# Activation split in eight steps behind evacuations, token-half pairs, an early pool for the first block product, and reordered phase-change loads

## The chip, the cores and the metric

The kernel runs on one core of a Trainium2 chip. The metric is device time in microseconds (us), the median of several executions. The profile is of one further execution, taken by the hardware profiler.

## What is computed

One layer on 1024 tokens of width 1024: an FFN, a mixer (stick-breaking attention beside RWKV-7), a second FFN, each between two RMS norms and added to the residual stream. The change touches the two FFNs alone (inner width 2816):

```python
def swiglu(x, w_gate, w_up, w_down):
    return (jax.nn.silu(x @ w_gate) * (x @ w_up)) @ w_down
# x = x + 0.5 * rmsnorm(swiglu(rmsnorm(x, pre_g), w_gate, w_up, w_down), post_g)
```

## The kernel before

Every fp32 product is three matmuls (`mm3`, L118 to L121): an operand is split into a rounded part "hi" and a remainder "lo" (fp32r), and hi x hi, hi x lo, lo x hi are added up in PSUM. Making hi is a cast on ACT (or POOL), making lo a subtraction on DVE (or POOL).

*Up-projection (`Ffn.up`).* The 2816 inner channels are 22 blocks of 128. Blocks 0 and 1 are done plainly (`plain_mm`, `plain_evac`), and their activations are stored, split, to DRAM (`hf`). Blocks 2 to 21 use a 2 x 2 Strassen scheme (Winograd's form) over halves of the depth, halves of the tokens and the gate and up weights: seven products n = 1..7 of 12 matmuls each instead of eight. `combine` makes the seven activation operands once, from the normed input (sums of 128x2048 on DVE: R, H, L). `prep(f)` makes a block's seven weight operands, hi and lo, on DVE (sums S), ACT and POOL (wh, wl); it is called one block ahead. `load(f)` brings the raw gate and up weights (r0, r1). `product(f)` runs the seven on PE in the order X n1, Z n2, DY n5, X n6, DW n4, X n7, DY n3. Three of them go to bank X one on top of the other: ACT must copy p out of it between n1 and n6, u between n6 and n7, and v after n7. Sums and the gated products on DVE then make the block's activations in both token halves.

*The split.* These activations are split again, for the down-projection, and stored. For blocks 2 to 17 two neighbouring blocks make one Strassen operand set of seven (`split_pair`, to `hs`); blocks 18 to 21 are split plainly (`split_plain`, to `hl`). Both are generators: `split_step()` runs one piece, at seven places in `product(f)`. A pair is queued after its odd block, so its steps run in the even block that follows. Whether an instruction keeps the place in which it is written is a scheduler's decision: it orders every engine's program ahead of time.

*Down-projection (`ffn_down`).* First the two plain blocks (`df`, 96 matmuls from `hf`, weights W split by POOL), then four groups of four blocks by Strassen (`prep(c)` makes the weights from four tiles B, with sums T, on POOL and ACT; PE runs `dX`, `dY`, `dZ`), then blocks 18 to 21 plainly. SP issues nearly all DMAs, in order: one that waits holds up all behind it.

Pools: `fu` holds the raw weights of even blocks, S, and the activations; `WP` those of odd blocks and most wh/wl pairs; `st` is one ring of six 128x512 tiles for hi, lo and one sum.

Of the kernel before, what the change touches and what calls it, by code (L numbers as in the profile page):

```python
# [30 lines left out]
def layer_kernel(ctx: ExitStack, tc: tile.TileContext, a: dict, out: bass.AP, dbg=None):  # L31
# [183 lines left out]
    class Ffn:  # L215
# [138 lines left out]
        def split(self, src, hi, lo, dst, eng=None):  # L354
            nc.scalar.copy(hi, src)
            nc.vector.tensor_tensor(lo, src, hi, op=ALU.subtract)
            for x, t in enumerate((hi, lo)):
                (eng or nc.sync).dma_start(dst(x).rearrange("i p t -> p i t"),
                                  t.bitcast(F32).rearrange("p (i t) -> p i t", t=P))

        def st(self, name, dt=F32R):
# [1222 lines left out]
```

## Time and profile before

| what | value |
|---|---|
| median of 3 runs | 2334.72 us (2334.41 to 2335.84) |
| the profiled execution | 2340.09 us, its span 2338.3 us |
| TensorE (PE) busy in the span | 2140.4 us, 92% |
| products of FFN1 on PE | 103.22 to 531.34 us |
| products of FFN2 on PE | 1664.94 to 2093.01 us |
| Strassen part of the down-projection begins | 570.01 us and 2133.24 us |

An engine's idle stretch counts only where PE waits for it. A timeline row gives the start, the length, engine, line, operation, output and input tiles with shapes, and in brackets the idle time before it and what ended that. Tile names lose their block numbers in the profile: f1u is u of any block of FFN1.

### The profile page before, as it was taken

How to read it: one execution, taken by the hardware profiler on the slowest of the kernel's cores; microseconds unless marked ns; L12 is line 12 of the kernel's file. 1: busy time of each engine (PE TensorE's matmuls, PEld its weight loads, DVE VectorE, ACT ScalarE, POOL GpSimd, SP SyncE). 2: the span in 40 equal slices, each digit the busy share in tenths (PEclk: the TensorE clock that was granted, in tenths of full speed). 3: DMA queues.
4: the chain of work that ended last, by engine and by line, in shares of the span. 5: the costliest groups of instructions: out<-in, count | busy, mean ns of one | idle time of the engine just before them, and what ended most of it. 6: DMA issues, size and time to landing. Idle time of an engine off the chain costs nothing. (4 is left out here: it accounts for less than half of the span.)

```text
span 2338.3 us, 30308 instructions
## 1 busy us (share of the span) xinstructions
PE 2140.4 (92%) x10976; PEld 1756.4 (75%) x10976; DVE 1296.4 (55%) x1900; ACT 823.3 (35%) x1429; POOL 1058.0 (45%) x899
## 2 busy tenths in 40 slices
PE   7689999997999999999999999898699999989998
PEld 5567777786888777677888887777577777767886
DVE  5765654641555655735526768556656546532555
ACT  4323333323112544324136657335233233332202
POOL 2266555557562354344311111221565555556742
PEclk8899999998999999999989889999899999999999
DMA  4244454448766353353665562442344545547765
GB/s 123 66 126 123 131 149 117 136 139 274 238 204 203 99 162 117 109 167 112 211 147 162 155 197 88 153 136 90 90 122 135 144 117 146 147 143 243 248 212 171
DMA packets 415476, 353.83 MB, mean 151 GB/s; under 512 B 35168, under 2 KB 337248, under 8 KB 415328
## 3 DMA queue, kind: packets, MB, share of 16 engines
q1 hardware_dynamic: 402512, 345.35, 49.5%
q10 hardware_dynamic: 12816, 6.56, 1.1%
q8 instruction: 87, 1.43, 0.3%
q14 instruction: 61, 0.50, 0.1%
HBM read 224.96 MB, written 126.88 MB: 150 GB/s over the span
## 5 line engine op out<-in xcount | busy, mean ns | idle before, releaser
L314 POOL TENSOR_TENSOR f1wl<-f1r,f1wh 128x512 fp32r<-128x512 f32 x100 | 138.9, 1400 | 101.4 <-ACT f1wh L311 98.1
L314 POOL TENSOR_TENSOR f2wl<-f2r,f2wh 128x512 fp32r<-128x512 f32 x100 | 138.7, 1398 | 94.1 <-ACT f2wh L311 90.9
L107 POOL TENSOR_SCALAR wh<-wr 128x1024 fp32r<-128x1024 f32 x55 | 64.9, 1180 | 243.9 <-PE wod L121 57.2
L108 POOL TENSOR_TENSOR wl<-wr,wh 128x1024 fp32r<-128x1024 f32 x55 | 136.9, 2491 | 21.2 <-PE f1dY L121 18.0
L512 DVE TENSOR_TENSOR f2acc<-f2dX,f2acc 128x512 f32<-128x512 f32 x64 | 44.3, 692 | 81.0 <-PE f2dX L121 81.0
L512 DVE TENSOR_TENSOR f1acc<-f1dX,f1acc 128x512 f32<-128x512 f32 x64 | 44.3, 691 | 79.4 <-PE f1dX L121 78.7
L313 POOL TENSOR_SCALAR f2wh<-f2r 128x512 fp32r<-128x512 f32 x60 | 46.2, 777 | 88.1 <-PE f2X L120 35.4
L313 POOL TENSOR_SCALAR f1wh<-f1r 128x512 fp32r<-128x512 f32 x60 | 46.1, 774 | 87.1 <-PE f1X L120 36.0
L458 DVE TENSOR_TENSOR f2y<-f2X,f2y 128x512 f32<-128x512 f32 x20 | 13.8, 691 | 115.9 <-ACT f2v L457 115.9
L458 DVE TENSOR_TENSOR f1y<-f1X,f1y 128x512 f32<-128x512 f32 x20 | 13.8, 691 | 115.8 <-ACT f1v L457 115.8
L1408 POOL TENSOR_SCALAR a_0B<-a_512B 128x1 f32<-128x1 f32 x32 | 14.1, 440 | 138.3 <-DVE a_512B L1409 110.3
L119 PE MATMUL pj<-x1X4h,wh 128*128 128x512 f32 x176 | 76.6, 435 | 0.0
L119 PE MATMUL pj<-x1X2h,wh 128*128 128x512 f32 x176 | 72.6, 412 | 0.6 <-DVE qkl L1119 0.5
L121 PE MATMUL pj<-x1X4h,wl 128*128 128x512 f32 x176 | 72.2, 410 | 0.0
L120 PE MATMUL pj<-x1X4l,wh 128*128 128x512 f32 x176 | 70.7, 402 | 0.0
L121 PE MATMUL pj<-x1X2h,wl 128*128 128x512 f32 x176 | 69.5, 395 | 0.0
L120 PE MATMUL pj<-x1X2l,wh 128*128 128x512 f32 x176 | 69.1, 393 | 0.0
L119 PE MATMUL f1X<-X_1h,f1wh 128*128 128x512 f32 x80 | 37.3, 466 | 25.4 <-ACT f1u L451 25.4
L119 PE MATMUL f2X<-x2X4h,f2wh 128*128 128x512 f32 x80 | 36.9, 461 | 23.4 <-ACT f2u L451 23.4
L314 POOL TENSOR_TENSOR f1wl<-f1S,f1wh 128x512 fp32r<-128x512 f32 x40 | 56.4, 1417 | 4.0 <-ACT f1wh L311 2.4
L314 POOL TENSOR_TENSOR f2wl<-f2S,f2wh 128x512 fp32r<-128x512 f32 x40 | 55.9, 1404 | 4.0 <-ACT f2wh L311 2.4
L540 POOL TENSOR_TENSOR f2dwl<-f2B,f2dwh 128x1024 fp32r<-128x1024 f32 x20 | 47.5, 2401 | 18.4 <-ACT f2dwh L539 18.4
(1472 smaller groups left out, 7247.2 us busy)
## 6 DMA issues: line engine op xcount, KB each, us to landing
f1ho<-f1hs_d SPq DMA_DIRECT2D x112, 256.0 KB, 4.0
f2ho<-f2hs_d SPq DMA_DIRECT2D x112, 256.0 KB, 3.3
f1hs_d<-f1sh SPq DMA_DIRECT2D x56, 256.0 KB, 2.8
f1hs_d<-f1sl SPq DMA_DIRECT2D x56, 256.0 KB, 2.5
f2hs_d<-f2sh SPq DMA_DIRECT2D x56, 256.0 KB, 2.8
f2hs_d<-f2sl SPq DMA_DIRECT2D x56, 256.0 KB, 2.5
wr<-in_w_in_dram SPq DMA_DIRECT2D x27, 512.0 KB, 3.9
f1r<-in_ffn_w_gate_dram SPq DMA_DIRECT2D x20, 512.0 KB, 4.4
```

Of the source, the lines that this page charges most:

```text
L107: nc.gpsimd.tensor_scalar(wh, raw, 1.0, 0.0, op0=ALU.mult, op1=ALU.add)
L108: nc.gpsimd.tensor_tensor(wl, raw, wh, op=ALU.subtract)
L119: nc.tensor.matmul(ps, lhsT=lh, rhs=rh, start=first, stop=False, **kw)
L120: nc.tensor.matmul(ps, lhsT=lh, rhs=rl, start=False, stop=False, **kw)
L121: nc.tensor.matmul(ps, lhsT=ll, rhs=rh, start=False, stop=last, **kw)
L313: nc.gpsimd.tensor_scalar(wh, src[n], 1.0, 0.0, op0=ALU.mult, op1=ALU.add)
L314: nc.gpsimd.tensor_tensor(wl, src[n], wh, op=ALU.subtract)
L458: nc.vector.tensor_tensor(y5, x, y5, op=ALU.add)
L512: nc.vector.tensor_tensor(quarter(tt, n), ps, quarter(tt, n), op=ALU.add)
L540: nc.gpsimd.tensor_tensor(wl, src[n], wh, op=ALU.subtract)
L1408: nc.gpsimd.tensor_scalar(B[:, w:w + 1], iv, 1.0, 0.0, op0=ALU.mult, op1=ALU.add)
```

## The change

- `split_pair` becomes a list of seven casts with the subtractions and sums one step behind, eight steps in all; its instructions and those of `split_plain` are kept in program order. `product` calls `split_step` at five places, each behind an evacuation.
- The ring `st` becomes three: `sh` (3), `sl` (2), `s1` (1); a block's activations are two 128x512 tiles (the former v and y) instead of one of 128x1024.
- A pair joins token tile i with i + 4 (halves) instead of 2i with 2i + 1, in the stores and in the down-projection.
- Raw weights of even blocks and S move to a pool `fr` that is open before the plain blocks; `load(2)` is issued on ACT's queue, and `prep(2)` is called before the last plain evacuations.
- In `ffn_down`, W, B's first tiles and all of hf are asked for at the top; hf gets a place of its own; eight hl stores move from ACT's queue to SP's. Five of the thirteen t4 tiles come from a pool that is opened later.

```diff
-            pool, tag = (WP, "wr") if f % 2 else (self.fu, "raw")
+            pool, tag = (WP, "wr") if f % 2 else (self.fr, "raw")
...
-                nc.sync.dma_start(t, w[:, :, c])
+                (nc.scalar if f == 2 else nc.sync).dma_start(t, w[:, :, c])
...
+        def hi(self, nm, n, src):
+            t = self.fu.tile("sh", f"{self.nm}h{nm}{n}", [P, HT], F32R)
+            tc.keep_in_program_order(nc.scalar.copy(t, src))
+            return t
+
+        def tt(self, dst, a_, b_, op):
+            tc.keep_in_program_order(nc.vector.tensor_tensor(dst, a_, b_, op=op))
...
+            steps = ((1, A11, (S, A21, A22, ALU.add)), (2, A12, (A21, A11, A21, ALU.subtract)),
+                     (4, A22, (A11, S, A11, ALU.subtract)), (5, S, (A12, A12, A11, ALU.subtract)),
+                     (7, A21, None), (6, A11, None), (3, A12, None))
+            held = None
+            for n, src, nxt in steps:
+                hi = self.hi(f, n, src)
+                if held is not None:
+                    lo(*held)
+                held = n, src, hi
+                if nxt is not None:
+                    self.tt(*nxt)
+                yield
+            lo(*held)
...
             self.mm(f, 1, "X")
+            self.mm(f, 2, "Z")
+            self.evac1(f)
             self.split_step()
-            self.mm(f, 2, "Z")
-            self.split_step()
-            self.evac1(f)
             y = self.mm(f, 5, "DY")
...
+            self.fr = Pool(self.nm + "r", dict(raw=2, S=1))
+            self.load(2)
             comb = self.combine()
...
             self.plain_mm(1, 1)
             next(comb)
+            self.prep(2)
             self.plain_evac(0, 1)
             self.plain_evac(1, 1)
             next(comb, None)
-            self.fu = Pool(self.nm + "u", dict(raw=2, S=1, wh=1, wl=1, tp=6, hv=2, st=6))
-            self.load(2)
+            self.fu = Pool(self.nm + "u", dict(wh=1, wl=1, tp=3, hv=6, sh=3, sl=2, s1=1))
             self.load(3)
-            self.prep(2)
...
+        W = [weight(F.wd[:, 0:2, n * 512:(n + 1) * 512], 2, 512, False) for n in range(2)]
         acc = [pl.t4(f"{nm}acc{tt}") for tt in range(NT)]
         rp = Pool(nm + "rp", dict(wh=6, wl=6, rw=5, T=2), "right")
+        B0 = blocks(0)
+        hp = Pool(nm + "hp", {}, "right")
+        hf = hp.const(f"{nm}hf", [P, NT, 2, 2, P], F32R)
+        for tt in range(NT):
+            nc.sync.dma_start(hf[:, tt].bitcast(F32), F.hf[tt])
...
-            a_, b_ = 2 * i, 2 * i + 1
+            a_, b_ = i, i + 4
```

ACT in block 14 (even) of FFN1 before, from the copy of p to that of u (f1sh are the split's casts, f1wh weight casts, f1hv activations):

```order
L434 COPY f1p14_2623<-f1X14_2586 128x512
L384 CAST f1sh79_2620<-f1hv13_2554 128x512
L384 CAST f1sh81_2646<-f1hv13_2554 128x512
L311 CAST f1wh_47_2569<-f1S15_2557 128x512
L436 ACTIVATE f1p14_2623<-f1p14_2623 128x512
L384 CAST f1sh83_2667<-f1s177_2601 128x512
L384 CAST f1sh85_2687<-f1hv12_2414 128x512
L447 COPY f1y14_2640<-f1DY14_2627 128x512
L384 CAST f1sh87_2709<-f1hv12_2414 128x512
L384 CAST f1sh89_2727<-f1hv13_2554 128x512
L311 CAST f1wh_48_2575<-f1r1_15_2446 128x512
L451 COPY f1u14_2661<-f1X14_2586 128x512
```

The same stretch of ACT in the change, where f1h121 is the cast of operand 1 of the pair that begins with block 12:

```order
L419 COPY f1p14_2603<-f1X14_2577 128x512
L312 CAST f1wh_47_2560<-f1S15_2548 128x512
L421 ACTIVATE f1p14_2603<-f1p14_2603 128x512
L368 CAST f1h121_2608<-f1v12_2364 128x512
L431 COPY f1y14_2624<-f1DY14_2611 128x512
L368 CAST f1h122_2626<-f1v13_2528 128x512
L312 CAST f1wh_48_2566<-f1r1_15_2426 128x512
L435 COPY f1u14_2645<-f1X14_2577 128x512
```

Of six split casts two are left between the two copies; the others went behind u or into the odd block.

DVE at the end of `combine` before (f1L4 and X1_1l are its last remainders, f1e the plain activations, f1S2 the first sum of block 2's weights):

```order
L266 TENSOR_TENSOR f1R2_580<-f1R3_581,f1R2_580 128x2048
L251 TENSOR_TENSOR f1L4_577<-f1R1_579,f1H4_576 128x2048
L356 TENSOR_TENSOR f1e0_1_647<-f1e0_1_647 128x512
L350 TENSOR_TENSOR f1e1_1_654<-f1pZ1_1_616,f1e1_1_654 128x512
L251 TENSOR_TENSOR X1_1l_129<-f1R2_580,X1_1h_128 128x2048
L356 TENSOR_TENSOR f1e1_1_654<-f1e1_1_654 128x512
L302 TENSOR_TENSOR f1S2_675<-f1r1_2_669 128x512
L303 TENSOR_TENSOR f1S2_675<-f1S2_675,f1r0_2_667 128x512
```

The same stretch of DVE in the change:

```order
L267 TENSOR_TENSOR f1R2_587<-f1R3_588,f1R2_587 128x2048
L252 TENSOR_TENSOR f1L4_584<-f1R1_586,f1H4_583 128x2048
L304 TENSOR_TENSOR f1S2_654<-f1S2_654,f1r0_2_505 128x512
L305 TENSOR_TENSOR f1r1_2_507<-f1r0_2_505,f1r1_2_507 128x512
L309 TENSOR_TENSOR f1r0_2_505<-f1r0_2_505,f1S2_654 128x512
L351 TENSOR_TENSOR f1e0_1_681<-f1pZ0_1_534,f1e0_1_681 128x512
L351 TENSOR_TENSOR f1e1_1_688<-f1pZ1_1_623,f1e1_1_688 128x512
L252 TENSOR_TENSOR X1_1l_129<-f1R2_587,X1_1h_128 128x2048
L357 TENSOR_TENSOR f1e0_1_681<-f1e0_1_681 128x512
L357 TENSOR_TENSOR f1e1_1_688<-f1e1_1_688 128x512
```

Block 2's sums (its first, f1S2 from r1_2, stands six rows above these) now come ahead of the last remainder and of the plain activations of the second token half.

SP at the change of phase of FFN1 before (wr are plain down weights, f1B the Strassen ones, f1hf the plain activations; the hl stores of blocks 20 and 21 are on ACT's queue):

```order
L104 DMA wr5_3810<-in_ffn1_w_down_dram 128x2x512
L104 DMA wr6_5199<-in_ffn1_w_down_dram 128x2x512
L104 DMA wr7_5211<-in_ffn1_w_down_dram 128x2x512
L526 DMA f1B000_3818<-in_ffn1_w_down_dram 128x2x512
L526 DMA f1B001_3820<-in_ffn1_w_down_dram 128x2x512
L526 DMA f1B011_3822<-in_ffn1_w_down_dram 128x2x512
L526 DMA f1B010_3824<-in_ffn1_w_down_dram 128x2x512
L526 DMA f1B100_4018<-in_ffn1_w_down_dram 128x2x512
L555 DMA f1hf0_3858<-f1hf_d_120 128x512
```

SP at the same place in the change:

```order
L105 DMA wr6_5183<-in_ffn1_w_down_dram 128x2x512
L105 DMA wr7_5195<-in_ffn1_w_down_dram 128x2x512
L362 DMA f1hl_d_122<-f1h200_3672 128x4x128
L362 DMA f1hl_d_122<-f1v20_3622 128x4x128
L362 DMA f1hl_d_122<-f1h201_3692 128x4x128
L362 DMA f1hl_d_122<-f1y20_3573 128x4x128
L501 DMA f1hf_3807<-f1hf_d_120 128x512 x8
L520 DMA f1B00_3800<-in_ffn1_w_down_dram 128x2x512
L362 DMA f1hl_d_122<-f1h210_3756 128x4x128
L362 DMA f1hl_d_122<-f1v21_3736 128x4x128
L362 DMA f1hl_d_122<-f1h211_3761 128x4x128
L362 DMA f1hl_d_122<-f1y21_3687 128x4x128
L520 DMA f1B01_3801<-in_ffn1_w_down_dram 128x2x512
```

hf moved ahead of B, and the four hl stores of block 21 stand between B's first tile and its other three.

## Rows read from the trace of the kernel before

**Rows 1.** the page's busy time, share of the span and instructions of each engine

```profile
PE 2140.4 (92%) x10976; PEld 1756.4 (75%) x10976; DVE 1296.4 (55%) x1900; ACT 823.3 (35%) x1429; POOL 1058.0 (45%) x899
```

**Rows 2.** PE's waits from 103 to 535 us: us in total, times, longest

```profile
PE f1X L119 <- ACT f1u L451: 25.4, 10, 3.0
```

**Rows 3.** PE's waits from 1660 to 2100 us

```profile
PE f2X L119 <- ACT f2u L451: 23.4, 9, 3.2
```

**Rows 4.** stretch: us, busy PE, PEld, DVE, ACT, POOL; clock, DMA share, GB/s

```profile
103.30:531.40 428.10, 400.11 (x1680) 325.29 (x1680) 243.14 (x293) 134.11 (x240) 259.75 (x222) 0.96 0.46 128
...
293.10:296.50 3.40, 3.33 (x9) 2.67 (x10) 2.46 (x3) 0.02 (x1) 1.31 (x1) 0.56 0.79 217
```

**Rows 5.** PE's timeline around one wait: start, us, what it is

```profile
287.46 0.39 PE L119 MATMUL f1DW<-f1H,f1wh 128*128 128x512 f32 x1
...
289.95 0.39 PE L121 MATMUL f1DW<-f1H,f1wl 128*128 128x512 f32 x1
293.17 0.79 PE L119 MATMUL f1X<-X_1h,f1wh 128*128 128x512 f32 x1 [2.83 <-ACT f1u L451]
293.76 0.63 PE L120 MATMUL f1X<-X_1l,f1wh 128*128 128x512 f32 x1
```

**Rows 6.** ACT's timeline in an odd block (one row), then an even one

```profile
268.62 0.59 ACT L451 COPY f1u<-f1X 128x512 f32<-128x512 f32 x1 [0.76 <-PE f1X L121]
...
287.57 0.64 ACT L436 ACTIVATE f1p<-f1p 128x512 f32<-128x512 f32 x1 [4.68 <-DVE f1p L435]
...
291.50 0.62 ACT L384 CAST f1sh<-f1hv 128x512 fp32r<-128x512 f32 x1 [1.26 <-DVE f1sl L389]
...
292.54 0.58 ACT L451 COPY f1u<-f1X 128x512 f32<-128x512 f32 x1
```

**Rows 7.** timelines of DVE (two rows) and POOL in that even block

```profile
285.16 1.77 DVE L404 TENSOR_TENSOR f1hv<-f1s,f1hv 128x512 f32<-128x512 f32 x1
286.86 0.68 DVE L435 TENSOR_TENSOR f1p<-f1Z,f1p 128x512 f32<-128x512 f32 x1
...
276.61 0.63 POOL L313 TENSOR_SCALAR f1wh<-f1S 128x512 fp32r<-128x512 f32 x1 [1.73 <-PE f1DY L120]
277.32 1.29 POOL L314 TENSOR_TENSOR f1wl<-f1S,f1wh 128x512 fp32r<-128x512 f32 x1
...
284.65 1.73 POOL L314 TENSOR_TENSOR f1wl<-f1S,f1wh 128x512 fp32r<-128x512 f32 x1
```

**Rows 8.** timelines where products start: PE, DVE, POOL; last PE in FFN2

```profile
103.22 0.79 PE L119 MATMUL f1X<-X_0h,f1wh 128*128 128x512 f32 x1 [16.98 <-POOL f1wh L313]
...
93.63 2.28 DVE L251 TENSOR_TENSOR X_1l<-f1R,X_1h 128x2048 fp32r<-128x2048 f32 x1
...
100.34 1.26 POOL L314 TENSOR_TENSOR f1wl<-f1r,f1wh 128x512 fp32r<-128x512 f32 x1 [74.71 <-ACT f1wh L311]
...
1664.94 0.80 PE L119 MATMUL f2X<-x2X2h,f2wh 128*128 128x512 f32 x1 [17.20 <-POOL f2wh L313]
```

**Rows 9.** the page's DMA issues: KB each, median us to landing

```profile
f1hs_d<-f1sh SPq DMA_DIRECT2D x56, 256.0 KB, 2.8
...
f1r<-in_ffn_w_gate_dram SPq DMA_DIRECT2D x20, 512.0 KB, 4.4
```

**Rows 10.** timelines where down-projections start: PE (four rows), POOL, ACT

```profile
543.16 0.76 PE L119 MATMUL f1df<-wh,f1hf 128*128 128x512 f32 x1 [11.82 <-DMA f1hf<-f1hf_d]
...
570.01 0.39 PE L119 MATMUL f1dX<-f1dwh,f1ho 128*128 128x512 f32 x1
...
2104.67 0.77 PE L119 MATMUL f2df<-wh,f2hf 128*128 128x512 f32 x1 [11.66 <-DMA f2hf<-f2hf_d]
...
2133.24 0.39 PE L119 MATMUL f2dX<-f2dwh,f2ho 128*128 128x512 f32 x1
...
537.78 2.34 POOL L529 TENSOR_TENSOR f1T<-f1B,f1B 128x1024 f32<-128x1024 f32 x1
...
551.91 1.04 ACT L539 CAST f1dwh<-f1B 128x1024 fp32r<-128x1024 f32 x1 [5.95 <-POOL f1B L536]
```

More of the change, by code (lines that the diff above doesn't have):

```diff
@@ L43, in __init__ @@
             self.bufs = bufs
+            self.more = None
         def close(self):
@@ L54, in t4 @@
         def t4(self, name, shape=None, dt=F32, tag="t4"):
-            return self.tile(tag, name, shape or [P, 1024], dt)
+            return (self.more or self).tile(tag, name, shape or [P, 1024], dt)
         def t2(self, name, shape=None, dt=F32, tag="t2"):
@@ L351, in plain_evac, with split, put @@
             self.split(hv, s.bitcast(F32R), hv.bitcast(F32R), lambda x: self.hf[4 * h:4 * h + 4, :, x, f, :])
-        def split(self, src, hi, lo, dst, eng=None):
+        def split(self, src, hi, lo, dst):
             nc.scalar.copy(hi, src)
             nc.vector.tensor_tensor(lo, src, hi, op=ALU.subtract)
-            for x, t in enumerate((hi, lo)):
-                (eng or nc.sync).dma_start(dst(x).rearrange("i p t -> p i t"),
+            self.put(dst, hi, lo)
+        def put(self, dst, *parts):
+            for x, t in enumerate(parts):
+                nc.sync.dma_start(dst(x).rearrange("i p t -> p i t"),
@@ L500, in up, with blocks @@
             self.fu.close()
+            self.fr.close()
     def ffn_down(pl, F, gb, post, half=None, nextx=None):
         nm = F.nm
+        def blocks(c):
+            f0 = FS + 4 * c
+            return [v2(rp.tile("rw", f"{nm}B{c}{x}", [P, 1024])) for x in range(4)]
+        v2 = lambda t: t.rearrange("p (k e) -> p k e", k=2)
+        W = [weight(F.wd[:, 0:2, n * 512:(n + 1) * 512], 2, 512, False) for n in range(2)]
         acc = [pl.t4(f"{nm}acc{tt}") for tt in range(NT)]
         rp = Pool(nm + "rp", dict(wh=6, wl=6, rw=5, T=2), "right")
+        B0 = blocks(0)
[3 more added lines that the diff above has]
+            nc.sync.dma_start(hf[:, tt].bitcast(F32), F.hf[tt])
         quarter = lambda tt, n: acc[tt][:, n * 512:(n + 1) * 512]
-        v2 = lambda t: t.rearrange("p (k e) -> p k e", k=2)
         nslot = [0]
@@ L518, in slot, with prep @@
             return [v2(pool.tile(t, f"{nm}d{t}{i}", [P, 1024], F32R)) for t in ("wh", "wl")]
-        def prep(c):
+        def prep(c, tiles):
             f0 = FS + 4 * c
-            first = slot()
             B = {}
-            for kh, e in ((0, 0), (0, 1), (1, 1), (1, 0)):
-                B[kh, e] = v2(rp.tile("rw", f"{nm}B{c}{kh}{e}", [P, 1024]))
+            for t, (kh, e) in zip(tiles, ((0, 0), (0, 1), (1, 1), (1, 0))):
+                B[kh, e] = t
                 nc.sync.dma_start(B[kh, e], F.wd[:, f0 + kh:f0 + kh + 4:2, e * 512:(e + 1) * 512])
@@ L548, in hload @@
             return ho
-        W = [weight(F.wd[:, 0:2, n * 512:(n + 1) * 512], 2, 512, False) for n in range(2)]
-        prep(0)
+        prep(0, B0)
         for tt in range(NT):
-            h2 = pl.tile("ho", f"{nm}hf{tt}", [P, 2, 2, P], F32R)
-            nc.sync.dma_start(h2.bitcast(F32), F.hf[tt])
+            h2 = hf[:, tt]
             for n in range(2):
@@ L627, in ffn_down @@
         EX[0] = None
+        pl.more.close()
         ex.close()
```

84 lines of the change are left out of this document (23 added, 61 removed).

## The prediction

> **What bounds the kernel now.** I first read the page's table of engines: TensorE (PE) is busy for 92% of the span, DVE 55%, POOL 45%, ACT 35% [rows 1]. So the time is PE's, and two things can shorten it: fewer matmuls (the change leaves their number alone) or fewer gaps between them. The second view is PE's waits in the two up-projections: on the ACT copy that makes u, FFN1 waits 10 times for 25.4 us [rows 2], FFN2 9 times for 23.4 us [rows 3]. The third is busy time by stretch: from 103.30 to 531.40 PE has 1680 matmuls in 428.1 us [rows 4].
>
> The floor: from 287.46 to 289.95 [rows 5] eleven distances of matmuls make 2.49 us, 0.2266 each. A block has 7 products of 12 matmuls, 84 x 0.2266 = 19.03 us; 20 blocks are 380.7 us. So the stretch is 47.4 us over its floor, 4.7 us for each of the ten even blocks. [Rows 5] show one of them: 2.83 us of waiting, then matmuls of 0.63 us instead of 0.39; the granted clock from 293.1 to 296.5 is 0.56 [rows 4], close to the lower of its two levels (1.2 and 2.4 GHz). A wait thus costs itself and nearly 2 us of slow matmuls.
>
> Why u is late: [rows 6] are ACT in that even block. X n6 ends where n4 begins, at 287.46; n4 takes 2.72 us, and then PE wants the bank again, but the copy of u only runs at 292.54. Before it stand silu (287.57, waiting for DVE's p), four casts of the split, y's copy and a weight cast; one cast at 291.50 waits for a DVE subtraction. DVE did split work first and came to p at 286.86, one step of it stretched to 1.77 us [rows 7]. In the odd block, where no split is queued, the copy stands at 268.62, in time.
>
> **The change, part by part.**
>
> *1. The split in eight steps, tied behind evacuations.* A pair of blocks still has 7 casts, 7 subtractions, 4 sums, and no matmul more or less. Between the copies of p and u, ACT had ten instructions in an even block, six of them split casts; now it has six with two. DVE makes p before it touches the split. Silu, cast, y's copy, cast and weight cast at 0.52 us (291.50 to 292.54 is two) put u 1.0 to 1.6 us ahead of PE's need, and no cast there waits for a subtraction of its own step. Five steps fall in the even block, three in the odd. So the ten waits go, with their slow matmuls. Bounds of what is left in an FFN: 0, or 1.5 us in each of 20 blocks, 30 us (the nearest row is the stretched DVE operation, 1.77 - 0.68 = 1.1 us, once or a little more per block). I take 3 us, near the low end, because the slack covers one such stretch.
>
> *The doubt in it: DVE beside POOL.* In [rows 7] POOL's subtraction takes 1.29 us, and 1.73 where DVE works too. A pair of blocks asks DVE for 23 operations with both inputs in SBUF (8 for the weights, 11 for the split, 4 products): 23 x 0.68 = 15.6 us. It asks POOL for 14 subtractions and 8 casts: 14 x 1.29 + 8 x 0.63 = 23.1 us. Sum 38.7 us, against PE's 38.07. In the old order the even block alone asks for 17 x 0.68 + 11.55 = 23.1 us against 19.03, which is why DVE came late there. Were the two engines wholly exclusive, a pair would take 0.7 us more than PE's floor. POOL's operation from 284.65 ends at 286.38, and DVE's from 285.16 ends 0.55 us after it. The Trainium skill ("SBUF — State Buffer", section "Who interferes with whom") says that two such operations exclude each other for a whole instruction; by that rule, the trace agrees at this place, and rival (b) below would hold.
>
> *2. Block 2 prepared early.* Today POOL's first subtraction for it stands at 100.34 and PE's first product at 103.22 after 16.98 us of waiting [rows 8]. The change issues its two loads on ACT's queue, among the last scalings of the input at about 67 us; with 4.4 us to land [rows 9] they are there at 72. POOL is idle, so what n1, n2, n5 and n4 need is ready before the plain blocks end at 103.22 - 16.98 = 86.24, and PE goes on at once. The price: four DVE operations of 0.6 us, all before the last sum, which ended at 95.91 [rows 8] and now ends near 99; only n7 reads it, now the last product of the block. X n6 waits for p's copy, behind two casts on ACT: 97.9 instead of 97.1, 0.9 us. Block 3's loads still stand behind hf's stores: last store near 100.5, landing 2.8 us and load 4.4 us [rows 9], cast and subtraction 0.63 + 1.29 [rows 7], so 109.6 where PE comes at 106.1: 3.5 us, and slow matmuls after it 1.6 us, by [rows 5]. Sum 6 us, of the old 17. Bounds 3 (loads land at once) and 11 (four DVE sums stretched by 1.1 us each). FFN1's products then end at 86.24 + 380.7 + 6 + 3 = 475.9 instead of 543.16 - 11.82 = 531.34 [rows 10]: 55.4 us. FFN2's plain part ends at 1664.94 - 17.20 = 1647.74 [rows 8]; 1647.74 + 389.7 = 2037.4 instead of 2104.67 - 11.66 = 2093.01: 55.6 us.
>
> *3. The start of the down-projection.* Now PE waits 11.82 us for hf, has 96 plain matmuls (floor 21.75 us) and comes to the Strassen part at 570.01, 38.7 us after the products; in FFN2 40.2 us [rows 10]. The change loads hf into a place of its own when n4 of the last block is over, 8 us before the end, so the hf wait goes. But only B's first tile is issued before the last hl stores; the other three stand behind them, and these wait for the block's evacuation, 6 us after the end: B lands 10.5 us after it. POOL's first T stood 6.4 us after the end, at 537.78, and each step takes 2.34 us: T moves 4 us later, and ACT's cast at 551.91 (20.6 us after the end), which waits for the fourth difference, to 24.6. PE's eleventh plain group needs an ACT copy behind that cast: 26.4, and its last five groups take 5 x 6 x 0.2266 = 6.8: 33.2 us after the end. Gain 5.5 and 7.0 us. Bounds: 0 (POOL's chain is late by all that PE gains) and 11.8 (the hf wait goes, nothing takes its place); the value lies between them, where the chain of rows puts it.
>
> Eight hl stores move from ACT's queue to SP's; the four of the last block are costed here by what stands behind them in SP's order. The Trainium skill ("DMA: Bandwidth & Descriptors", section "Issuing engines are not separate DMA queues") has it that the choice of engine saves only issue time; by that, the move is free and this gain is nearer 11.8 than 5.5 us. No row of before shows the stores on SP; I keep the order's answer.
>
> *4. The rest.* Token-half pairs change where stores go, not how many there are. Buffers shrink: 3 for hi and 2 for lo, where six were shared. Two lo buffers turn in two steps, 7.6 us in an even block; a store lands in 2.8 us [rows 9], so I cost it at nothing. The mixer, the Strassen part and the tail keep their instructions.
>
> **Sum.** 55.4 + 55.6 + 5.5 + 7.0 = 123.5 us. The profiled execution took 2340.09 us (its span is 2338.3), so 2216.6; the median, 2334.72, is 5.4 us less: 2211 us.
>
> **Rivals.**
> - *(a) The wait only moves.* A cast held up by DVE or POOL keeps u late once a pair. 19 waits at 4.4 us (the stretch's 47.4 us less the 3 assumed, over ten) are 84 us, less the 6 taken: 2289; with half of them, 2250. For it: operations of 1.77 us [rows 7]. Against: in the odd block the same neighbours let u through in time.
> - *(b) DVE and POOL are the floor:* 0.7 us over 20 pairs, and weights that reach PE late by as much again: 28 us, less the 6 taken: 2233. For it 38.7 against 38.07; against it, that the sums at 0.68 count each start-up in full.
> - *(c) The down start gains nothing*, POOL's chain being its bound: 12.5 us, 2224.
> - *(d) Slower.* Fewer buffers under a tied order: a store that lands late blocks DVE's next subtraction, behind which p and the products stand, so PE waits in all blocks. A lo buffer is free for 7.6 us less 1.1 for subtraction and issue; past 6.5 us of landing, each us is paid four times a pair, two in a block. It decides at 123.5 / 40 = 3.1 us a block, a landing of 8.05 us; at 8.5 us it is 160 us, 2371. Against it: 2.8 us on the row, and DMA's share of 0.46 [rows 4].
>
> **Chances.** Forecast 0.55, (a) 0.14, (b) 0.14, (c) 0.11, (d) 0.06. A measurement of this kernel tells 0.2%, 4.7 us, from no change. Only (d) is not faster, and nearly all of it is slower: faster 0.93, same 0.02, slower 0.05. The range's low end is all low bounds: 2 x 3 for the starts, 2 x 3 for the stretches, 11 for the down starts, 2188. Its high end takes (b), (c) and half of (a), with the start's upper bound of 2 x 5: about 2262.
>
> **What would show it.** Right: no wait on u over 1 us, clock 0.98 or more over the products, the first product at 86.3, one wait near 3.5 us in block 3, products ending near 476, the Strassen part 33 us later. Wrong: PE waiting once a pair on an ACT line, POOL's weights as PE's releaser in mid-stretch, or the Strassen part over 38 us after the products.

## The result, and the profile after

The changed kernel takes 2236.85 us (median of 4 runs, 2232.27 to 2241.4) against 2335.28 for the kernel before on the same chip: a ratio of 0.9576, 95% interval 0.9553 to 0.9599. It is 98 us faster. 2211 was predicted, a gain of 123.5; the range (2188 to about 2262) holds the result, but a fifth of the gain is missing. The profiled execution took 2238.49 us, 101.6 less than that of before.

The page's table of engines, as in [rows 1]:

```profile
PE 2106.6 (94%) x10976; PEld 1730.0 (77%) x10976; DVE 1336.3 (60%) x1900; ACT 821.3 (37%) x1429; POOL 1113.9 (50%) x899
```

The same matmuls, 34 us less busy time on PE (fewer slow ones), and 56 us more on POOL for the same 899 instructions. Something on POOL became longer.

Busy time by stretch (us; PE, PEld, DVE, ACT, POOL; granted clock, DMA share, GB/s), first blocks 2 and 3 of FFN1 up to the late u of block 3, then the rest of block 3 and blocks 4 to 21, against [rows 4]:

```profile
94.86:142.90 48.04, 39.39 (x145) 30.45 (x145) 23.69 (x22) 10.54 (x19) 35.79 (x28) 0.86 0.31 88
143.00:493.30 350.30, 350.30 (x1533) 288.82 (x1534) 240.84 (x272) 123.46 (x222) 232.03 (x195) 0.99 0.54 151
```

In the second stretch PE is busy for all of its 350.30 us, at clock 0.99; blocks 4 to 21 take 19.04 to 19.11 us each, where the floor is 19.03. The waits on u of [rows 2, 3] are gone there. In block 10, which is even, PE ends n6 at 276.24 and wants the bank again at 278.96. DVE makes p before it turns to the split, and u's copy is over at 277.36, 1.6 us ahead of PE's need (DVE's timeline, then one row of ACT's):

```profile
271.07 0.69 DVE L420 TENSOR_TENSOR f1p<-f1Z,f1p 128x512 f32<-128x512 f32 x1 [1.10 <-PE f1Z L122]
271.67 1.70 DVE L372 TENSOR_TENSOR f1s<-f1y,f1y 128x512 f32<-128x512 f32 x1
...
276.78 0.58 ACT L435 COPY f1u<-f1X 128x512 f32<-128x512 f32 x1
```

The miss lies in the first stretch. PE's waits in FFN1 (us in total, times, longest):

```profile
PE f1X L120 <- POOL f1wh L314: 12.0, 2, 7.9
PE f1X L120 <- ACT f1u L435: 4.3, 1, 4.3
PE f1df L120 <- ACT f1acc L551: 3.7, 2, 3.3
PE f1dZ L121 <- POOL f1dwl L533: 3.6, 1, 3.6
```

PE's timeline (start, us): the first product of block 2 and of block 3, the late u of block 3, the first matmul behind the products, the start of the down-projection up to dX of its Strassen part, and in FFN2 block 2 and dX:

```profile
94.86 0.80 PE L120 MATMUL f1X<-X_0h,f1wh 128*128 128x512 f32 x1 [7.90 <-POOL f1wh L314]
...
121.26 0.79 PE L120 MATMUL f1X<-X_0h,f1wh 128*128 128x512 f32 x1 [4.11 <-POOL f1wh L314]
...
142.75 0.80 PE L120 MATMUL f1X<-X_1h,f1wh 128*128 128x512 f32 x1 [4.28 <-ACT f1u L435]
...
494.10 0.39 PE L120 MATMUL f1df<-wh,f1hf 128*128 128x512 f32 x1
...
513.83 0.80 PE L121 MATMUL f1dZ<-f1dwl,f1ho 128*128 128x512 f32 x1 [3.59 <-POOL f1dwl L533]
...
520.02 0.55 PE L120 MATMUL f1df<-wh,f1hf 128*128 128x512 f32 x1 [3.27 <-ACT f1acc L551]
...
528.58 0.39 PE L120 MATMUL f1dX<-f1dwh,f1ho 128*128 128x512 f32 x1
...
1599.94 0.79 PE L120 MATMUL f2X<-x2X2h,f2wh 128*128 128x512 f32 x1 [7.83 <-POOL f2wh L314]
...
2033.10 0.39 PE L120 MATMUL f2dX<-f2dwh,f2ho 128*128 128x512 f32 x1
```

Block 2 takes 121.26 - 94.86 = 26.4 us and block 3 29.7. With the 7.9 us ahead of them, that is 25.9 us over the floor (7.9 + 7.4 + 10.6) where 6 were predicted.

The same start before the change (PE's timeline: blocks 3 and 4 begin):

```profile
126.33 0.39 PE L119 MATMUL f1X<-X_0h,f1wh 128*128 128x512 f32 x1
...
149.66 0.39 PE L119 MATMUL f1X<-X_0h,f1wh 128*128 128x512 f32 x1
```

From 103.22 [rows 8], block 2 took 23.1 us and block 3 23.3. With the 17.0 us ahead of them the start was 25.4 us over the floor. So the change gained nothing there (25.6 became 23.8 in FFN2); what it gained in the products lies in blocks 4 to 21. What POOL did, and DVE beside it:

```profile
73.68 21.13 POOL L314 TENSOR_SCALAR f1wh<-f1r 128x512 fp32r<-128x512 f32 x1 [48.37 <-PE f1pX L121]
94.89 2.50 POOL L315 TENSOR_TENSOR f1wl<-f1r,f1wh 128x512 fp32r<-128x512 f32 x2
```

```profile
72.63 2.28 DVE L256 TENSOR_TENSOR f1R<-f1R,f1R 128x2048 f32<-128x2048 f32 x1
...
93.05 0.68 DVE L304 TENSOR_TENSOR f1S<-f1S,f1r 128x512 f32<-128x512 f32 x1
93.65 0.68 DVE L305 TENSOR_TENSOR f1r<-f1r,f1r 128x512 f32<-128x512 f32 x1
97.43 1.09 DVE L309 TENSOR_TENSOR f1r<-f1r,f1S 128x512 f32<-128x512 f32 x1 [3.10 <-POOL f1wl L315]
```

A cast that took 0.63 us in [rows 7] lasts 21.13 here (21.05 in FFN2). It ends at 94.81, 0.5 us after DVE's unbroken row of two-input operations has paused at 94.3. None of DVE's operations in that row is lengthened. So POOL was idle, as the prediction said, and still did nothing.

What follows is the queue behind it. In SP's order a load for block 4 stands first; it takes the place of block 2's raw weights and waits 33.8 us for POOL to have read them. Behind it stand hf's stores, whose data DVE had ready at 104.63. Behind these stand block 3's loads, which wait until the stores have landed at 113.98 and 114.56 (SP's timeline; the first row is block 4's load, the last block 3's):

```profile
107.66 0.37 SPq L281 DMA_DIRECT2D f1r<-in_ffn_w_gate_dram  x1
108.12 2.92 SPq L362 DMA_DIRECT2D f1hf_d<-f1e  x4
...
113.99 0.37 SPq L281 DMA_DIRECT2D f1r<-in_ffn_w_gate_dram  x1
```

Block 3's weights land at 120.51 and 122.20. POOL then has block 3's and 4's operands to make in a row, DVE's sums wait for POOL, and p of block 3 waits on DVE behind them (DVE's timeline):

```profile
138.87 1.09 DVE L309 TENSOR_TENSOR f1r<-f1r,f1S 128x512 f32<-128x512 f32 x1 [2.42 <-POOL f1wl L315]
139.88 0.68 DVE L420 TENSOR_TENSOR f1p<-f1Z,f1p 128x512 f32<-128x512 f32 x1
```

That is the late u at 142.75. From block 4 on, the products run as predicted.

*The account of the 101.6 us.* FFN1's products end 37.2 us earlier (531.34 to 494.10), FFN2's stretch from the plain part to the end of the products is 40.2 us shorter. The down-projection's start, from the products' end to the first dX, takes 34.5 and 35.9 us instead of 38.7 and 40.2 [rows 10]: 4.2 and 4.3. The way from FFN1's dX to the end of FFN2's plain blocks, nearly all mixer, is 14.2 us shorter, and the rest 1.5. But in after seven Strassen matmuls (six of dZ, one of dY) run ahead of dX, between 509.85 and 516.76 in FFN1, and in before none. At the floor's distance they are 1.6 us of work, which then no longer stands behind dX. So the starts gained 5.8 and 5.9 us, the way 12.6, and the rest nothing. The 12.6 us are mixer, whose instructions the change leaves alone. They show most in one stretch, the same work in before and in after:

```profile
1278.00:1390.00 112.00, 104.27 (x809) 92.76 (x807) 75.58 (x135) 67.63 (x135) 18.06 (x46) 0.88 0.58 173
```

```profile
1233.00:1334.40 101.40, 94.92 (x807) 84.04 (x806) 75.31 (x134) 67.46 (x135) 18.91 (x46) 0.97 0.65 190
```

10.6 us, and the granted clock went from 0.88 to 0.97.

### The profile page after: what moved, and what is told of

Same layout as the page of the kernel before. It is cut to its first block, busy times and chain, and to the rows that moved or that the text cites. A ratio compares the mean times of both kernels' runs of the same rounds, so it can differ in the third digit from the quotient of the medians.

```text
span 2236.7 us, 30262 instructions
## 1 busy us (share of the span) xinstructions
PE 2106.6 (94%) x10976; PEld 1730.0 (77%) x10976; DVE 1336.3 (60%) x1900; ACT 821.3 (37%) x1429; POOL 1113.9 (50%) x899
## 4 chain that ended last, share of the span: by engine, by line
PE 76%; DVE 9%; issue 4%; POOL 4%; ACT 3%; DMA 2%; SPq 0%; DVEq 0%; POOLq 0%; ACTq 0%
PE pj L120 3%; PE pj L122 3%; PE pj L121 2%; PE f1X L120 2%; PE f2X L120 2%; PE f1X L122 2%; PE f1X L121 2%; PE f2X L122 2%; PE f2X L121 2%; PE f1DY L120 2%; PE f2DY L121 2%; PE f2DY L122 2%; PE f1DY L122 2%; PE f1DY L121 2%; PE f2DY L120 1%
## 5 line engine op out<-in xcount | busy, mean ns | idle before, releaser
L314 POOL TENSOR_SCALAR f1wh<-f1r 128x512 fp32r<-128x512 f32 x60 | 68.0, 1139 | 119.6 <-PE f1pX L121 48.4
L314 POOL TENSOR_SCALAR f2wh<-f2r 128x512 fp32r<-128x512 f32 x60 | 68.0, 1138 | 110.5 <-PE f2pX L121 40.9
L1402 POOL TENSOR_SCALAR a_0B<-a_512B 128x1 f32<-128x1 f32 x32 | 15.4, 481 | 132.0 <-DVE a_512B L1403 98.4
L315 POOL TENSOR_TENSOR f2wl<-f2S,f2wh 128x512 fp32r<-128x512 f32 x40 | 62.3, 1568 | 1.7
L315 POOL TENSOR_TENSOR f1wl<-f1S,f1wh 128x512 fp32r<-128x512 f32 x40 | 62.3, 1568 | 1.7
L533 POOL TENSOR_TENSOR f1dwl<-f1B,f1dwh 128x1024 fp32r<-128x1024 f32 x20 | 47.7, 2412 | 18.9 <-ACT f1dwh L532 18.9
L120 PE MATMUL wod<-wh,ymh 128*128 128x512 f32 x128 | 51.1, 399 | 1.1 <-DVE woacc L192 0.9
L122 PE MATMUL wod<-wh,yml 128*128 128x512 f32 x128 | 50.2, 395 | 0.1
L121 PE MATMUL wod<-wl,ymh 128*128 128x512 f32 x128 | 50.1, 392 | 0.0
```

The source lines that it names most:

```text
L120: nc.tensor.matmul(ps, lhsT=lh, rhs=rh, start=first, stop=False, **kw)
L121: nc.tensor.matmul(ps, lhsT=lh, rhs=rl, start=False, stop=False, **kw)
L122: nc.tensor.matmul(ps, lhsT=ll, rhs=rh, start=False, stop=last, **kw)
L314: nc.gpsimd.tensor_scalar(wh, src[n], 1.0, 0.0, op0=ALU.mult, op1=ALU.add)
L315: nc.gpsimd.tensor_tensor(wl, src[n], wh, op=ALU.subtract)
L533: nc.gpsimd.tensor_tensor(wl, src[n], wh, op=ALU.subtract)
```

## The experiments

The measure used below, beside the time, is the *product stretch*: from the last plain matmul to the last product of an FFN. Its floor is 381 us.

| kernel | FFN1, us | FFN2, us | median, us | ratio to before [95%] |
|---|---|---|---|---|
| before | 445.1 | 445.3 | 2335.28 | |
| changed | 407.3 | 405.2 | 2236.85 | 0.9576 [0.9553, 0.9599] |
| e1 early pool undone | 405.7 | 405.3 | 2242.34 | 0.9608 [0.9571, 0.9646] |
| e2 old down start | 406.0 | 406.9 | 2251.47 | 0.9641 [0.9611, 0.9671] |
| e3 block 2 off POOL, early loads | 393.6 | 393.6 | 2215.46 | 0.9484 [0.9452, 0.9516] |
| e5 one PSUM read in the row | 405.8 | 404.2 | 2233.68 | 0.9581 [0.9544, 0.9617] |
| e7 e3, p2 first | 396.6 | 396.5 | 2220.64 | 0.9521 [0.9477, 0.9565] |
| e8 e7, block 4 later | 396.0 | 396.5 | 2221.45 | 0.9514 [0.9480, 0.9547] |
| e9 block 2 off POOL, nothing else | 398.5 | 397.1 | 2221.48 | 0.9516 [0.9480, 0.9553] |

e1 to e4 ran on one chip, e5 to e7 on a second, e8 and e9 on a third, each with its own runs of before. Two runs are traces of one execution each: e4, 2332.63 us, and e6, 2234.32 us.

**e1: is the early pool worth anything?** Block 2's loads and operands go back behind the combinations; the split and the down start stay.

```diff
-            self.fr = Pool(self.nm + "r", dict(raw=2, S=1))
-            self.load(2)
...
-            self.prep(2)
...
+            self.fr = self.fu
+            self.load(2)
             self.load(3)
+            self.prep(2)
```

> The changed kernel with block 2's loads and preparation put back behind the combine; split, pairs and down start as changed. Theory A (in the change POOL's first cast for block 2 is held off for 21 us by DVE's unbroken row of sums with two SBUF inputs, which delays block 2, hf's stores and block 3 in turn): the early pool gains nothing; first product near 104 us, FFN1's products end at 493 +- 3 as in the change (494.1), time within 6 us of the changed kernel's 2237. Theory B (the early pool is worth the 8.4 us by which the first product starts earlier, and the losses in blocks 2 and 3 have other causes): products end 8 to 10 us later in each FFN, 2253 to 2257 us.

The first product starts 9.5 us later than in the changed kernel (PE's timeline):

```profile
104.36 0.80 PE L120 MATMUL f1X<-X_0h,f1wh 128*128 128x512 f32 x1 [17.34 <-POOL f1wh L314]
```

but blocks 2 and 3 then take 23.2 and 21.9 us, and the products end at 492.5, before the changed kernel's 494.1. The early pool is worth nothing net: what it gains at the start of block 2 is lost in blocks 2 and 3. FFN2 shows the same, 23.1 and 21.9 us.

**e2: the reordered loads.** `ffn_down` as before, with the token halves kept, and eight hl stores back on ACT's queue.

```diff
-        hf = hp.const(f"{nm}hf", [P, NT, 2, 2, P], F32R)
-        for tt in range(NT):
-            nc.sync.dma_start(hf[:, tt].bitcast(F32), F.hf[tt])
...
-        prep(0, B0)
+        W = [weight(F.wd[:, 0:2, n * 512:(n + 1) * 512], 2, 512, False) for n in range(2)]
+        prep(0)
         for tt in range(NT):
-            h2 = hf[:, tt]
+            h2 = pl.tile("ho", f"{nm}hf{tt}", [P, 2, 2, P], F32R)
+            nc.sync.dma_start(h2.bitcast(F32), F.hf[tt])
```

> The changed kernel with the old start of the down-projection (hf behind B, hl stores of blocks 20 and 21 on ACT's queue). Theory A (the reordered loads are worth 4.2 us in FFN1 and 4.3 in FFN2, as the distance from the products' end to the Strassen part fell from 38.7 to 34.5 and from 40.2 to 35.9): the distance is 38 to 40 again, 2243 to 2248 us. Theory B (hf's wait is hidden by POOL's chain anyway, and the distance fell because the products end in another order): distance stays at 34 to 36, 2236 to 2239 us.

PE's longest wait behind FFN1's products, and its first Strassen matmul:

```profile
PE f1df L120 <- DMA f1hf<-f1hf_d: 13.5, 1, 13.5
```

```profile
531.67 0.39 PE L120 MATMUL f1dX<-f1dwh,f1ho 128*128 128x512 f32 x1
```

The hf wait is back, and dX comes 39.6 and 39.8 us after the products instead of 34.5 and 35.9: 5.1 and 3.9 us. The seven matmuls stand behind dX again, so the loads are worth 6.7 and 5.5 us. The median is 3.5 us above the expected band, which left these 2 x 1.6 us out.

**e3: block 2 without POOL.** All of block 2's casts on ACT and its subtractions on DVE, written between the token combinations; block 3's loads ahead of them, and the activations of the plain blocks' second token half in a place of their own, so that the loads need not wait for them.

```diff
+            def W(*ns):
+                for n in ns:
...
+                    (K if n not in (3, 7) else lambda x: x)(nc.scalar.copy(sl[n][0], src[n]))
+                for n in ns:
+                    tt(sl[n][1], src[n], sl[n][0], op=ALU.subtract)
...
             tt(r3, *f32(3), op=ALU.add)
+            tt(S1, A21, A22, op=ALU.add)
+            W(1, 2)
```

> The changed kernel with block 2's weight operands made on ACT and DVE alone (none on POOL), DVE's sums in a fixed order, the last plain activations in a tile of the combine's ring, so that block 3's weights can load early. Theory A (POOL kept out by DVE): PE goes from the plain blocks to the first product without a wait, near 87 us; products end near 472, 20 us earlier than in the change, in each FFN: 2197 us; POOL's first cast for block 3 is again long wherever DVE has no gap. Theory B (the first product waits for the weights' loads or a slot, not for POOL's port): first product at 94 to 95 again, products end 490 to 494, 2230 to 2237 us.

PE goes on without a wait, and meets one in block 2 (PE's timeline, then ACT's around it):

```profile
86.67 0.39 PE L120 MATMUL f1X<-X_0h,f1wh 128*128 128x512 f32 x1
...
104.83 0.79 PE L120 MATMUL f1X<-f1H,f1wh 128*128 128x512 f32 x1 [7.12 <-ACT f1p L461]
```

```profile
101.36 1.90 ACT L253 CAST X_1h<-f1R 128x2048 fp32r<-128x2048 f32 x1 [2.41 <-DVE f1R L248]
103.16 0.61 ACT L306 CAST f1wh<-f1r 128x512 fp32r<-128x512 f32 x1
103.68 0.61 ACT L349 CAST f1wh<-f1r 128x512 fp32r<-128x512 f32 x1
104.20 0.57 ACT L461 COPY f1p<-f1X 128x512 f32<-128x512 f32 x1
```

The product stretch is 13.7 and 11.6 us shorter than in the changed kernel, and the time, 2215.46 us, is the shortest of all. Theory A is right about the first product, but not about the price: the products end at 480.2, not near 472, and 2197 us was expected.

**e4: how long is POOL held beside DVE?** The kernel before, with two idle casts and memsets on POOL in the row of combinations.

```diff
+            for _ in range(2):
+                nc.gpsimd.memset(pt, 0.0)
+                nc.gpsimd.tensor_scalar(pt, self.X[1][0][:, 7, :].bitcast(F32), 1.0, 0.0, ...)
```

> The kernel before, with four POOL instructions added during the combine that nothing depends on: memset 128x512, cast 128x512, memset, cast (the cast reads a part of the normed input). Theory A (DVE's rows of sums hold POOL off until DVE has an operation without a second SBUF input): the memsets take 0.5 us or less, the first cast is held until DVE's operation from PSUM at 76.4 us (3 to 5 us long), the second from there to DVE's next one, at 92 to 93 us: 15 us or more. The time stays at 2335 +- 4. Theory B (the 21 us were POOL's own: code, slot or input): both casts 0.6 us, beside the sums or not.

POOL's timeline:

```profile
69.72 2.01 POOL L256 TENSOR_SCALAR f1pt<-X_1h 128x512 f32<-128x512 f32 x1 [43.75 <-ACT X_1h L165]
71.79 0.53 POOL L255 MEMSET f1pt<- 128x512 f32 x1
72.40 1.95 POOL L256 TENSOR_SCALAR f1pt<-X_1h 128x512 f32<-128x512 f32 x1
```

Each cast waited for the DVE operations that ran when it came (at 69.72 one of two inputs and a short one that reads PSUM, at 72.40 one of two inputs), the memset for none. Neither expectation came true: DVE's row alone doesn't hold a cast for 15 us, and it isn't harmless either.

**e5: break the row.** One copy of 128 columns from PSUM is added to DVE's row.

```diff
             tt(r12, *f32(7), op=ALU.add)
+            pt = rp.tile("pt", f"{self.nm}pt", [P, P])
+            nc.vector.tensor_copy(pt, self.ps[0, 1][0][:, 0:P])
             tt(r1, r12, r1, op=ALU.subtract)
```

> The changed kernel with one small copy added to VectorE's row of sums: 128 columns of a PSUM bank into a spare tile, after the third sum, at about 75 us, so that between two operations with both inputs in SBUF stands one that reads PSUM. In the changed kernel GpSimd's first cast of block 2 starts at 73.68 and lasts 21.13 us, to 0.5 us after that row. Theory A: the cast is held by the unbroken row. Then it ends at 75 to 77 us instead of 94.8, GpSimd and VectorE alternate afterwards, block 2's first product starts at 87 to 89 us instead of 94.86, and the products end 5 to 9 us earlier in each FFN: 2219 to 2227 us. Rival B: the cast waits for its data, its slot or something else that the copy doesn't touch. Then it still ends near 94.8 us and the time stays within 2 us of the changed kernel's 2237. Chances 0.6 and 0.4.

POOL's timeline, then DVE's:

```profile
74.39 1.83 POOL L316 TENSOR_SCALAR f1wh<-f1r 128x512 fp32r<-128x512 f32 x1 [48.75 <-PE f1pX L121]
76.30 4.90 POOL L317 TENSOR_TENSOR f1wl<-f1r,f1wh 128x512 fp32r<-128x512 f32 x2
81.17 2.66 POOL L316 TENSOR_SCALAR f1wh<-f1S 128x512 fp32r<-128x512 f32 x1
```

```profile
75.65 0.28 DVE L257 COPY f1pt<-f1pX 128x128 f32<-128x128 f32 x1
...
85.89 5.99 DVE L252 TENSOR_TENSOR f1L<-f1R,f1H 128x2048 fp32r<-128x2048 f32 x2
```

The cast's end moves from 94.81 to 76.22, 0.3 us after the copy: theory A's mechanism, in both FFNs. From there the two engines alternate, and PE goes on at 87.51 without a wait. But its price was wrong: block 2 now takes 32.9 us, and the product stretch is 1.5 and 1.0 us shorter than in the changed kernel, not 5 to 9. While they alternate, two of DVE's operations take 5.99 us instead of 4.49, one of POOL's casts 2.66 instead of 0.63, and the second of block 2's sums, at the end of the row, starts at 99.51 instead of 93.05. So here the work of the two engines added up, whichever went first.

**e6: is it the operand?** The changed kernel with four small idle casts on POOL, three of tokens, one of block 2's raw weights.

```diff
+            for src in 3 * [self.X[1][0][:, 7, 0:P].bitcast(F32)] + [self.raw[2][0][:, 0]]:
+                nc.gpsimd.memset(pt, 0.0)
+                nc.gpsimd.tensor_scalar(pt, src, 1.0, 0.0, ...)
```

> The changed kernel with four idle casts of 128 columns on GpSimd ahead of the real one, each behind a memset of its scratch tile: three read the normalized tokens and write plain float32, the fourth reads block 2's raw weights; then comes the real cast, float32 to rounded float32. The first is ready at about 70 us, where VectorE's row has begun. Theory A, the row: the first two get in as in the probe (about 2 us each) and one of the later ones, whichever it reads, is held to the end of the row, 15 to 20 us. Rival B, the operand: the three that read tokens take 2.3 us at most each, however late, and only one that reads raw weights, or the one that writes rounded values, is held. Rival C: none is held over 5 us once GpSimd has been working, and the first product starts at 87 to 90 us. Chances 0.45, 0.25, 0.3.

The three of tokens ran before the row began and tell nothing. The fourth, and the real cast behind it, in FFN1 and FFN2 (POOL's timeline):

```profile
71.95 0.30 POOL L257 TENSOR_SCALAR f1pt<-f1r 128x128 f32<-128x128 f32 x1 [9.92 <-DMA f1r<-in_ffn_w_gate_dram]
73.32 21.23 POOL L318 TENSOR_SCALAR f1wh<-f1r 128x512 fp32r<-128x512 f32 x1 [1.07 <-PE f1pX L121]
...
1572.47 1.66 POOL L257 TENSOR_SCALAR f2pt<-f2r 128x128 f32<-128x128 f32 x1 [19.76 <-DMA f2r<-in_ffn_w_gate_dram]
1575.21 1.83 POOL L318 TENSOR_SCALAR f2wh<-f2r 128x512 fp32r<-128x512 f32 x1 [1.08 <-PE f2pX L121]
```

The same cast with the same operands is held for 21.23 us in one FFN and for 1.83 in the other, so the operand is not the cause (rival B falls). What differs is the POOL operation before it: 0.30 us, at a moment when DVE reads PSUM, against 1.66, which had waited. Neither A nor C came out as forecast in both: the real cast was held in FFN1 and let in at once in FFN2. FFN2, where POOL got in early, gained as little as e5: a stretch of 404.5 us.

**e7: the copy of p2 first.** e3, with products 1 and 2 of block 2 and the copy of p2 written ahead of the last combinations, and the split of the plain blocks' second half behind them.

```diff
+            next(comb)
+            self.mm(2, 1, "X")
+            self.mm(2, 2, "Z")
+            p2 = self.tp[2] = self.S1.rearrange("p k c -> p (k c)")
+            tc.keep_in_program_order(nc.scalar.copy(p2, self.ps[2, "X"]))
             next(comb, None)
```

> The version of e3 (block 2's operands on ScalarE and VectorE instead of GpSimd, block 3's loads early) with two more edits: products 1 and 2 of block 2 and the copy of p2 are written ahead of the last part of the token combinations, so that ScalarE does that copy before its casts for n7 and n3; and the second half's split of blocks 0 and 1 comes behind the combinations. In e3 block 2 takes 29.9 us against 19.0, with one wait of 7.12 us on that copy. Theory: the wait falls to under 2 us; what is late next is the seventh combination (VectorE ends it at 106 us in e3, 104 to 105 here), so block 2 takes 24 to 26 us, the products of each FFN end 4 to 6 us earlier, and the time is 2203 to 2209 us against e3's 2215. Rival: what is saved is lost again to the operands of n7 and n3, block 2 still takes 28 us or more, and the time is 2211 to 2216.

The 7.12 us on p2 went; 4.78 on y's copy and 3.97 on u's in block 3 came. Block 2 takes 26.6 us (29.9 in e3), block 3 26.8 (20.5). That is nearest to the rival: what is saved is lost again, and 3 us of the product stretch more. But block 2 takes less than the rival's 28 us, and the time is above its 2216.

**e8: block 4 behind p3.** e7, with `prep(4)` called behind the p add of block 3.

```diff
+            if f in (2, 3):
+                self.prep(f + 1)
```

> The version of e7 with one edit: block 4's operands are written behind block 3's p add, not ahead of it. In e7 block 2 took 26.6 us (4.78 of it one wait on the copy of y) and block 3 26.8 us, 3.97 of it a wait on the copy of u, which stood behind a p add that VectorE did at 128.63, after sums for block 4 that wait for GpSimd. Theory: without those sums ahead of it the p add is done by 121 us, the wait goes, block 3 takes 20 to 22 us, the products of each FFN end 4 to 6 us earlier than in e7 (477 to 479 us in FFN 1; 480.0 in e3), and the time is 2208 to 2213 us on a chip where e7 takes 2220. Rival: block 4's operands are late in turn, block 4 takes 22 us or more instead of 19.0, and the time stays within 3 us of e7's.

The scheduler kept the order that the edit was to change; DVE's timeline still has block 4's sums ahead of the p add (L469):

```profile
125.72 1.09 DVE L341 TENSOR_TENSOR f1S<-f1r 128x512 f32<-128x512 f32 x1 [1.18 <-POOL f1wl L353]
...
128.44 0.68 DVE L343 TENSOR_TENSOR f1r<-f1r,f1r 128x512 f32<-128x512 f32 x1
129.04 0.68 DVE L469 TENSOR_TENSOR f1p<-f1Z,f1p 128x512 f32<-128x512 f32 x1
```

The wait is 3.96 us as in e7, and the run tells nothing about either theory.

**e9: off POOL, and nothing else.** Two places of the changed kernel.

```diff
-                if n in (2, 6, 7):
+                if n in (2, 6, 7) or f == 2:
                     nc.scalar.copy(wh, src[n])
...
-                nc.gpsimd.tensor_tensor(wl, src[n], wh, op=ALU.subtract)
+                (nc.vector if f == 2 else nc.gpsimd).tensor_tensor(wl, src[n], wh, op=ALU.subtract)
```

> The changed kernel with one edit: block 2's casts are all on ScalarE and its subtractions on VectorE, where the code has them, behind the row of combinations; loads, slots and everything else are as in the changed kernel. It asks how much of e3's 14 us an FFN comes from taking this work off GpSimd and how much from e3's order. Theory, two thirds: the first product still starts at 94 to 96 us, since VectorE comes to the first subtraction only at the end of its row, but nothing is lengthened afterwards: block 2 takes 21 to 24 us instead of 26.4 and block 3 22 to 25 instead of 29.7, the products end at 483 to 488 us in FFN 1 (494.1 in the changed kernel, 480.0 in e3), 2216 to 2227 us. Rival, one third: block 3's late loads decide, it still takes 28 us or more, the products end at 490 to 494 and the time is within 8 us of the changed kernel's.

From 86.42 PE does eight matmuls that need only the hi parts of the weights, which ACT made, with waits of 2.49 and 1.97 us for parts of the token operands, and then waits for DVE's first lo parts of the weights (PE's timeline):

```profile
94.71 0.80 PE L122 MATMUL f1X<-X_0h,f1wl 128*128 128x512 f32 x1 [1.01 <-DVE f1wl L315]
```

From there block 2 needs 19.2 us for its other 76 matmuls, 2 us over their floor: DVE's subtractions take 0.70 us each and nothing is lengthened, as the theory had it. Block 3 is over its band at 27.9 us, as in the rival, but not for the rival's reason: its loads land at 110.98 and 112.66, some 9.5 us earlier than in the changed kernel, and PE doesn't wait for its weights. 5.5 us are a wait on u, behind a p that DVE makes at 130.65, after block 4's sums. The products end at 484.9, and the time is 2221.48 us, both inside the theory's band. So 8.8 and 8.1 us of e3's 13.7 and 11.6 come from taking the work off POOL. The rest came with e3's order and early loads, which no run parts.

## Why the prediction was right, and where it was not

*The split (part 1): right from block 4 on, but with too large a sum.* Blocks 4 to 21 run at 19.04 to 19.11 us with no wait; of the 3 us left over for each FFN 0.6 were needed. The step that failed is "4.7 us for each of the ten even blocks". The ten waits of [rows 2] lie in blocks 2, 3 and the eight even blocks 4 to 18. Blocks 2 and 3 have no split step of a pair queued, and were 8.4 of the 47.4 us over the floor; in e1, which has the new split and the old start, they take 23.2 and 21.9 us, still 7.0 over it. So of the 44.4 us that the prediction took here in FFN1 (47.4 less 3), 39.0 were to be had, and 38.4 came. That the order of the split did it is read from the trace, u's copy 1.6 us ahead, where 1.0 to 1.6 were predicted. No run takes the order back without the smaller rings and the token halves that came with it.

The doubt in part 1, rival (b), is refuted in the steady state: an exclusive pair would cost 0.7 us over 20 pairs, and the 350.30 us above are all PE.

*Block 2 (part 2): wrong.* The step that failed is "POOL is idle, so what n1, n2, n5 and n4 need is ready before the plain blocks end", with its "Sum 6 us, of the old 17"; 25.9 us stayed, and even the upper bound of 11 was too low. The prediction counted DVE beside POOL for the steady blocks and left it out here, where DVE's row runs without a pause from 72.63 to 94.33. The bound it took (four sums stretched by 1.1 us) is the cost to DVE; POOL's own delay was not priced. The runs show a part of the cause: with the work off POOL and nothing else changed, the product stretch is 16 to 18 us over its floor (e9), not 24 to 26; with POOL merely let in early the gain is 1.0 to 1.5 us (e5). So POOL's work beside DVE's row cost 8.8 and 8.1 us. e9 keeps the wait for operands from the end of DVE's row, and a block 3 that is 8.9 us over the floor, with a late u. e3 shortens the two together, so what each of them costs is not shown.

Block 3's term failed too. Its weights were forecast ready at 109.6, behind a last store "near 100.5"; that store went out at 110.05, behind block 4's load, and landed in 4.5 us, and the weights landed at 122.20. That PE's wait for them is 4.1 us, near the 3.5 forecast, is luck: PE came 11 us late as well.

The Trainium skill ("SBUF — State Buffer", section "Who interferes with whom") says that issue order decides who blocks, and that whoever is first holds the shared pair for its whole instruction. The start of the row agrees: DVE's operation at 72.63 came before POOL's cast at 73.68. The rest doesn't: eleven more of DVE's, all begun after the cast, went ahead of it.

The products' stretches fell short by 55.4 - 37.2 = 18.2 and 55.6 - 40.2 = 15.4 us: 33.6 us, more than the whole difference between 123.5 and 101.6, which the mixer hides in part.

*The down start (part 3): right in its steps.* ACT's cast behind the fourth difference was forecast 24.6 us after the products and stands at 518.44, 24.3 after them. The last five plain groups were forecast at 26.4; they begin at 520.02, 25.9 after the products. They take 8.6 us (9.4 in FFN2) instead of 6.8, at a granted clock of 0.80 (0.71) behind PE's waits of 3.6 and 3.3 us. Hence 34.5 and 35.9 us to dX instead of 33.2; but seven Strassen matmuls had run before, which the prediction didn't foresee. The gain is 5.8 and 5.9 us, and e2 gives 6.7 and 5.5, where 5.5 and 7.0 were predicted. POOL's first T stands at 504.25, 10.2 us after the end, and waits for B's load, as the chain of rows had it (POOL's timeline):

```profile
504.25 2.40 POOL L523 TENSOR_TENSOR f1T<-f1B,f1B 128x1024 f32<-128x1024 f32 x1 [2.17 <-DMA f1B<-in_ffn_w_down_dram]
```

The Trainium skill ("DMA: Bandwidth & Descriptors", section "Issuing engines are not separate DMA queues") says that the choice of engine saves only issue time. The prediction took from it that the stores' move is free and the gain near 11.8 us, and that did not come: in SP's order B's other tiles stand behind the stores of block 21, which go out at 496.19 to 498.05, and the first of them goes out at 499.58. No run moves the stores alone. Rival (c) fell too.

*The rivals (a) and (d)* did not happen: from block 4 on no wait on u recurs, and a store lands in 3.3 us instead of 2.8, far from 8. The range's high end is summed wrongly: by the prediction's own prices, (b) 22, (c) 12.5, half of (a) 39 and the starts 10 us make about 2294, not 2262; the result is inside either.

*What was in no part:* the 12.6 us of the mixer. The way from FFN1's dX to the last plain matmul of FFN2 takes 1059.7 to 1067.8 us in the eight profiles of variants of the changed kernel and 1063.2 in the changed one. In the two profiles with the old FFN (before and e4) it takes 1077.3 and 1070.9, in them with the seven matmuls, 1.6 us. The stretch shown above, the same matmuls each time, runs at clock 0.88 in before, 0.92 in e4, 0.94 in e1, e3 and e9, 0.97 in the changed kernel and 1.00 in e5, in 112.1 to 98.9 us. So a part of the 12.6 us is the spread from one execution to the next; whether the rest is caused by the change is open. If none of it is, the result would be nearer 2250 without it, and the miss is larger than it looks: that the time came as near to 2211 as it did is then in part luck.

## What to carry to other kernels

An idle engine is free only if nothing that it needs is held by another: before work is moved onto POOL, read what DVE does in that very stretch, and count DVE's operations with two inputs in SBUF and POOL's that read SBUF as one queue. To win time there, take the work to an engine outside the pair (here ACT, for the casts) or take it out of the stretch; letting POOL in earlier only moved the wait (e5). And look at what is queued behind work that is pulled forward, the stores and the next loads: here they stayed late, and e1, without the early pool, ends as early. Last, before waits are booked to one cause, see which blocks they lie in: two of the ten had another.

## What the runs showed of the hardware

- A POOL operation that reads SBUF can be held for 21.13 us by DVE operations of 0.68 and 2.28 us each, with no gap between them in the trace; a memset in such a row took 0.53 us and was not held (e4).
- In all places seen here, the first POOL operation that met such a row got in when DVE paused or did something that reads PSUM (94.3 in the changed kernel; the 0.28 us copy in e5). An operation that followed one which had itself waited was held for only one DVE operation (e4, e6 in FFN2, e5), and then the two alternated. What decides this was not settled further.
- A DMA that waits holds those behind it on SP: hf's stores, ready at 104.63, went out at 108.12, behind a load that had waited for POOL until 107.66.
- The granted clock of the same instructions in the mixer was 0.88, 0.92, 0.94, 0.97 and 1.00 in five profiles, 112.1 to 98.9 us: as much as some of the changes made here.
